# A fifth output tile beside the first four in the output projections behind the mixers, and wider spacing of the last heads of the differential attention

## The chip, the cores and the metric

The kernel runs on one core of one Trainium2 chip. The metric is the device time of one execution in microseconds (us). Each time below is the median of several executions; the time before is the median of 3, 1430.43 us (1430.12 to 1432.36).

## The reference

A stack of two transformer layers and one hybrid layer on 256 tokens of width 1024, in float32. The first two layers put 16 meta tokens in front, so that they work on 272 rows. Cut to what matters here:

```python
for i in range(2):                                    # 272 rows
    h = h + 0.5 * rmsnorm(swiglu(rmsnorm(h, g[0]), ...), g[1])
    m = neighborhood_attention(...) if i == 0 else diff_attention(...)
    h = h + rmsnorm(m, g[3])                          # m = concat(heads) @ w_o
    h = h + 0.5 * rmsnorm(swiglu(rmsnorm(h, g[4]), ...), g[5])
x = h[:, 16:]
x = x + rms_norm(concat(attention, mlstm) @ w_out, g_mix_post)
x = x + rms_norm(square(relu(rms_norm(x, g) @ w_up)) @ w_down, g_mlp_post)
```

Each of the three mixers (neighbourhood attention, differential attention, and attention beside an mLSTM) ends in a 1024 x 1024 output projection, followed by an RMS norm over the row and by the next layer's up projection. These three projections are what the change touches.

## The kernel before, in words

Activations lie transposed, as eight blocks of 128 features by 272 (or 256) token columns. A weight matrix comes from HBM in pieces of 1 MB (256 output columns), three of which fit in the ring of raw pieces `wr`. Each piece makes two parts of 128 columns. A part is split into two float32r halves: ScalarE copies it (`wh`, L156), VectorE subtracts the copy from the raw piece (`wl`, L168). Seven parts can be held. `mm3` (L390 to L395) multiplies one 128-row block of one part with one block of the activations in three matmuls (high with high, high with low, low with high), a triple below; an output tile of the projection is eight triples in one PSUM accumulator `pm`.

The order in every queue is the order in which the code is written (`tc.manual_schedule()`); `Weights.pump` (L180) puts the splits between the other work, and `low` (L162) issues the next 1 MB transfer on SyncE's queue as soon as both parts of a raw piece are split. `high` (L137) refuses a part that is more than seven beyond the last part given back by `W.done`.

While a mixer's projections run, the attention is a generator in `bg_list`; each `bg()` runs it up to its next `yield`. `proj_out` (L688) starts before the attention has ended: it takes four output tiles at once and goes over the eight blocks of the attention's output (`Oh`, `Ol`) as these become ready, two `bg()` per block. Then it evacuates the four tiles (two ScalarE instructions each, the square for the norm, L379 or L387, and the scaled copy, L603 or L606; VectorE adds up the squares, L388) and does tiles 4 to 7 one after the other with `gemm`, each evacuated behind its matmuls. `pump` calls stand between the evacuations. At the end `post.finish` (L609) makes the row's 1/rms: sums over partitions on TensorE (L344), two small VectorE steps, a power on GpSimd (L349), transposes on TensorE; `start_phase` (L465) fills TensorE meanwhile with matmuls whose result is not used (L476, twice nine).

In the differential attention `da_attention` (L1204) unit u is one of 16 pairs of head and query tile; behind unit 15 the loop has four more turns for the work that is left: `values(u-3)` (L1240), `scale(u-3)` (L1253, VectorE), and `emit` (L1259 to L1261), which transposes a head's two scaled tiles and writes `Oh` and `Ol`. In these four turns each step has one `yield`.

Of the kernel before, what the change touches and what calls it, by code (L numbers as in the profile page):

```python
# [79 lines left out]
class Weights:  # L80
# [111 lines left out]
    def next(self):  # L192
        p = self.n_next
        while self.n_split <= p:
            if self.n_high <= p:
                before = self.n_high
                self.high()
                assert self.n_high > before
            self.low()
        self.n_next += 1  # L200
        return self.parts[p]
# [8 lines left out]
def block_kernel(ctx: ExitStack, tc: tile.TileContext, a, out):  # L210
# [13 lines left out]
    def nm(s):  # L224
        uid[0] += 1
        return f"{s}_{uid[0]}"
# [13 lines left out]
    def keep():  # L240
        ring_next[0] = (ring_next[0] + 1) % len(ring_blocks)
        return ring_blocks[ring_next[0]]

    def small(shape, s="s"):
        n = int(np.prod(shape[1:]))
        return tp.tile(shape, F32, name=nm(s), tag="s4" if n <= 4 else "s64", bufs=40 if n <= 4 else 6)

    def ps_mm():
        return pp.tile([128, T], F32, name=nm("pm"), tag="mm", bufs=6)

    def ps_s(shape=(128, T)):
        return pp.tile(list(shape), F32, name=nm("ps"), tag="mm", bufs=6)

    def ps_t(shape=(128, T)):
        return pp.tile(list(shape), F32, name=nm("pt"), tag="t", bufs=2)


    W = Weights(nc, wp)
# [53 lines left out]
    x = a["x"][0].rearrange("(t p) f -> p t f", p=128)  # L312
# [77 lines left out]
    def mm3(ps, w, k, x, j, cols, start, stop):  # L390
        wh, wl = w
        xh, xl = x
        pe.matmul(ps, wh[:, k, :], xh[:, j, cols], start=start, stop=False)  # L393
        pe.matmul(ps, wh[:, k, :], xl[:, j, cols], start=False, stop=False)  # L394
        pe.matmul(ps, wl[:, k, :], xh[:, j, cols], start=False, stop=stop)  # L395
# [4 lines left out]
    def bg(n=1):  # L400
        for _ in range(n):
            while bg_list:
                try:
                    next(bg_list[0])
                    break
                except StopIteration:
                    bg_list.pop(0)

    def gemm(ps, x, cols, kb=8, start=True, stop=True, inside={}):
        w = W.next()  # L410
        for k in range(kb):
            mm3(ps[:, cols], w, k, x, k, cols, start and k == 0, stop and k == kb - 1)
            if k in inside:
                inside[k]()
            if k in bg_at[0]:
                bg()
        W.done()
# [269 lines left out]

    def proj_out(post, x, order=range(8)):  # L688

        c = post.cols  # L690
        w = [W.next() for _ in range(4)]
        ps = [ps_mm() for _ in range(4)]
        for n, k in enumerate(order):
            while k not in ready:
                assert bg_list
                bg()
            W.flush()
            for q in range(4):
                mm3(ps[q][:, c], w[q], k, x, k, c, n == 0, n == 7)
                if q % 2:  # L700
                    bg()
        while bg_list:
            bg()
        bg_at[0] = (3,)
        ready.clear()
        W.done(4)
        for q in range(4):
            post.evac(ps[q], q)
            if q % 2:
                W.pump(1 if q == 1 else 2)  # L710
        for j in range(4, 8):
            p = ps_mm()
            gemm(p, x, c)
            post.evac(p, j)
            if j < 6:
                W.pump()
# [200 lines left out]
    def softmax(ps, parts, n, sm):  # L917


        lg, mn = tmp("lg"), 3.0e38  # L920
        for cols, bias in parts:
            hi, mn = mn, small([128, 1])
            dve.tensor_tensor_reduce(out=lg[:, cols], in0=ps[:, cols], in1=bias, scale=-1.0, scalar=hi,
                                     op0=OP.add, op1=OP.min, accum_out=mn)
        e = keep()
        act.activation(e[:, 0:n], lg[:, 0:n], AF.Exp, bias=mn, scale=-1.0, accum_out=sm)
        return e
# [40 lines left out]
    def available(n):  # L968

        while progress["units"] <= n:  # L970
            yield
# [226 lines left out]
    def token_rms(o):  # L1198

        q, ss = tmp("osq"), small([128, 1])  # L1200
        act.activation(q[:, 0:128], o, AF.Square, accum_out=ss)
        return ss

    def da_attention():  # L1204

        vp, A, AT, OS, normed, sums, first = {}, {}, {}, {}, {}, {}, {}

        def scores(u):
            hd, qt = divmod(u, 2)
            A[u] = []  # L1210
            sums[u] = small([128, 2])
            for s in range(2):
                ps = ps_s()
                pe.matmul(ps, kq[64 * s:64 * s + 64, hd % 4, QT[qt]], kq[64 * s:64 * s + 64, 4 + hd % 4, :],
                          start=True, stop=True)
                u0 = 128 * (1 - qt)
                A[u].append(softmax(ps, [(ALL, t5b[hd // 4][:, hd % 4, u0:u0 + T])], T, sums[u][:, s:s + 1]))

        def weights(u):
            e0, e1 = A[u]  # L1220
            sm, r, x = sums.pop(u), small([128, 2]), small([128, 1])
            dve.reciprocal(r, sm)
            dve.scalar_tensor_tensor(x, r[:, 1:2], sm[:, 0:1], nlam, op0=OP.mult, op1=OP.mult)
            dve.scalar_tensor_tensor(e0, e1, x, e0, op0=OP.mult, op1=OP.add)
            A[u], first[u] = e0, r[:, 0:1]

        def turn(u):
            if u % 2 == 0:
                AT[u // 2] = ring[0].tile().rearrange("p (t k q) -> p t k q", t=2, k=3)
            q = A.pop(u)  # L1230
            p = ps_t((128, 3, 128))
            for i, x in enumerate((0, 128, 144)):
                pe.transpose(p[:, i, :], q[:, x:x + 128], ident)
            act.activation(AT[u // 2][:, u % 2], p, AF.Copy)

        def values(u):
            hd, qt = divmod(u, 2)
            o = ps_s((128, 128))
            for k in range(3):
                pe.matmul(o, AT[hd][:, qt, k, :], vp[hd][:, k, :], start=k == 0, stop=k == 2)  # L1240
            ss = token_rms(o)
            m, r, r0 = small([128, 1]), small([128, 1]), first.pop(u)
            dve.scalar_tensor_tensor(m, ss, r0, r0, op0=OP.mult, op1=OP.mult)
            dve.tensor_scalar(m, m, 1.0 / 128, EPS, op0=OP.mult, op1=OP.add)
            pool.tensor_tensor(r, m, mhalf[:, 0:1], op=OP.pow)
            normed[u] = o, r0, r

        def scale(u):
            hd, qt = divmod(u, 2)
            o, r0, r = normed.pop(u)  # L1250
            if qt == 0:
                OS[hd] = keep()
            dve.tensor_scalar(OS[hd][:, qt * 128:qt * 128 + 128], o, r0, r, op0=OP.mult, op1=OP.mult)  # L1253

        def emit(hd):
            p = ps_t((128, 256))
            t = OS.pop(hd)
            for qt in range(2):
                pe.transpose(p[:, qt * 128:qt * 128 + 128], t[:, qt * 128:qt * 128 + 128], ident)  # L1259
            act.activation(Oh[:, hd, GRID], p, AF.Copy, scale=gsub)  # L1260
            dve.scalar_tensor_tensor(Ol[:, hd, GRID], p, gsub, Oh[:, hd, GRID].bitcast(F32),  # L1261
                                     op0=OP.mult, op1=OP.subtract)
            ready.add(hd)

        def turn_v(hd):
            vp[hd] = vp_ring[hd % len(vp_ring)]
            transpose_pair(vp[hd], vT.pop(hd))

        def v_step(u):
            if u % 2 == 0 and 2 <= u < 18:  # L1270
                while u // 2 - 1 not in vT:
                    yield
                turn_v(u // 2 - 1)

        for u in range(16 + 4):
            if u % 2 and u >= 5:
                emit((u - 5) // 2)
            if 3 <= u < 19:
                values(u - 3)
            if 2 <= u < 18:  # L1280
                turn(u - 2)
            yield
            if u < 16:
                yield from available(u)
                scores(u)
                yield
            yield from v_step(u)
            if 3 <= u < 19:
                scale(u - 3)
            if u < 16:  # L1290
                weights(u)
                yield

    mixer(norm, post, da_evac, da_attention, GRID, lambda n: None)
    post = Post(gains(1, 3), GRID)
# [22 lines left out]
    c = GRID  # L1318
# [355 lines left out]
    for n in range(2):  # L1674
        ps = [ps_s((128, 512)) for _ in range(2)]
        for i in range(12 if n else 16):
            w = W.next()
# [9 lines left out]
    w = [W.next() for _ in range(4)]  # L1687
# [34 lines left out]
```

## Time and profile before

| | |
|---|---|
| median of 3 executions | 1430.43 us |
| the profiled execution | 1431.22 us, of which its span 1429.4 us |
| TensorE matmul busy | 1408.2 us (99%) |
| VectorE, ScalarE, GpSimd busy | 893.7, 750.2, 168.1 us |
| mean granted TensorE clock | 0.998 of full speed |
| moved by DMA | 234.41 MB, mean 164 GB/s |

TensorE has matmuls in nearly every stretch, but its busy time contains the matmuls that only fill it (L476). An engine's row in the timeline shows start, length, line, operation, out<-in, and in brackets the idle time before it and what released it. The three projections run from 328 to 358 us (272 columns, neighbourhood attention), 877 to 907 us (256 columns, differential attention) and, in the hybrid layer, up to 1236 us (256 columns).

### The profile page before, as it was taken

How to read it: one execution, taken by the hardware profiler on the slowest of the kernel's cores; microseconds unless marked ns; L12 is line 12 of the kernel's file. 1: busy time of each engine (PE TensorE's matmuls, PEld its weight loads, DVE VectorE, ACT ScalarE, POOL GpSimd, SP SyncE). 2: the span in 40 equal slices, each digit the busy share in tenths (PEclk: the TensorE clock that was granted, in tenths of full speed). 3: DMA queues.
4: the chain of work that ended last, by engine and by line, in shares of the span. 5: the costliest groups of instructions: out<-in, count | busy, mean ns of one | idle time of the engine just before them, and what ended most of it. 6: DMA issues, size and time to landing. Idle time of an engine off the chain costs nothing.

```text
span 1429.4 us, 26895 instructions
## 1 busy us (share of the span) xinstructions
PE 1408.2 (99%) x11068; PEld 1357.6 (95%) x11068; DVE 893.7 (63%) x1668; ACT 750.2 (52%) x1333; POOL 168.1 (12%) x185
## 2 busy tenths in 40 slices
PE   9999999999999999999999999999999999999997
PEld 9999999899999999999999888999999888899886
DVE  6776447664865544955546785776555877686542
ACT  5554346666554444644445564664444565676441
POOL 1325001010221200212100001031100000000000
PEclk9999999999999999999999999999999999999999
DMA  7875552352575554555553352375554543275650
GB/s 250 271 251 172 179 185 66 124 167 90 167 229 172 168 180 148 175 180 177 163 182 99 119 177 89 112 244 184 188 178 131 177 129 108 89 234 179 221 177 30
DMA packets 219528, 234.41 MB, mean 164 GB/s; under 512 B 5313, under 2 KB 209894, under 8 KB 219214
## 3 DMA queue, kind: packets, MB, share of 16 engines
q1 hardware_dynamic: 218206, 227.38, 49.2%
q0 software_dynamic: 656, 4.94, 1.1%
q8 instruction: 87, 1.43, 0.4%
q10 hardware_dynamic: 544, 0.38, 0.1%
q14 instruction: 35, 0.29, 0.1%
HBM read 231.62 MB, written 5.13 MB: 166 GB/s over the span
## 4 chain that ended last, share of the span: by engine, by line
PE 91%; DVE 6%; ACT 2%; DMA 1%; issue 1%; POOL 0%; DVEq 0%; POOLq 0%; ACTq 0%; SPq 0%
PE pm L393 24%; PE pm L395 24%; PE pm L394 23%; PE ps L1645 2%; PE ps L1644 2%; PE ps L1646 2%; PE pm L506 2%; DVE wl L168 2%; PE pm L502 2%; PE pm L503 1%; DMA wr<-in_da_w_qkv_dram 1%; PE pt L344 1%; PE pt L1013 1%; PE pm L540 1%; PE ps L1022 1%
## 5 line engine op out<-in xcount | busy, mean ns | idle before, releaser
L168 DVE TENSOR_TENSOR wl<-wr,wh 128x1024 fp32r<-128x1024 f32 (+1 forms) x430 | 514.3, 1204 | 122.9 <-ACT wh L156 122.2
L393 PE MATMUL pm<-xh,wh 128*128 128x272 f32 (+1 forms) x1992 | 581.4, 292 | 2.2 <-DVE Ol L421 2.2
L395 PE MATMUL pm<-xh,wl 128*128 128x272 f32 (+1 forms) x1992 | 570.4, 286 | 0.0
L394 PE MATMUL pm<-xl,wh 128*128 128x272 f32 (+1 forms) x1992 | 568.5, 285 | 0.0
L156 ACT ACTIVATE wh<-wr 128x1024 fp32r<-128x1024 f32 (+1 forms) x430 | 440.7, 1033 | 194.0 <-PE pm L394 112.9
L393 PEld LDWEIGHTS pm<-xh,wh 128*128 128x128 f32 x1992 | 376.0, 189 | 11.2 <-issue 9.4
L395 PEld LDWEIGHTS pm<-xh,wl 128*128 128x128 f32 x1992 | 375.9, 189 | 0.1
L394 PEld LDWEIGHTS pm<-xl,wh 128*128 128x128 f32 x1992 | 375.6, 189 | 0.1
L395 PE MATMUL pm<-mh,wl 128*128 128x272 f32 (+1 forms) x704 | 202.2, 287 | 0.0
L393 PE MATMUL pm<-mh,wh 128*128 128x272 f32 (+1 forms) x704 | 202.1, 287 | 0.0
L394 PE MATMUL pm<-ml,wh 128*128 128x272 f32 (+1 forms) x704 | 201.5, 286 | 0.0
L650 POOL TENSOR_TENSOR sr<-sl,rb 128x272 f32<-128x272 f32 (+1 forms) x88 | 104.5, 1192 | 320.1 <-ACT sl L648 320.1
L395 PEld LDWEIGHTS pm<-mh,wl 128*128 128x128 f32 x704 | 132.7, 188 | 0.0
L394 PEld LDWEIGHTS pm<-ml,wh 128*128 128x128 f32 x704 | 132.6, 188 | 0.0
L393 PEld LDWEIGHTS pm<-mh,wh 128*128 128x128 f32 x704 | 132.6, 188 | 0.0
L420 ACT ACTIVATE mh<-m 128x272 fp32r<-128x272 f32 (+1 forms) x88 | 37.7, 428 | 117.8 <-DVE m L655 117.6
L655 DVE TENSOR_TENSOR m<-pm,sr 128x272 f32<-128x272 f32 (+1 forms) x88 | 38.3, 435 | 80.5 <-PE pm L395 74.8
L648 ACT ACTIVATE sl<-gq 128x272 f32<-128x272 f32 (+1 forms) x88 | 36.9, 427 | 95.8 <-DVE gq L646 95.6
L349 POOL TENSOR_TENSOR s<-s,mhalf 128x3 f32<-128x3 f32 (+1 forms) x15 | 19.1, 1274 | 558.4 <-DVE s L362 336.1
L646 DVE TENSOR_TENSOR gq<-pm,rb 128x272 f32<-128x272 f32 (+1 forms) x88 | 37.6, 435 | 71.6 <-PE pm L395 69.0
L388 DVE TENSOR_TENSOR accf<-accf,sq 128x272 f32<-128x272 f32 (+1 forms) x42 | 18.3, 436 | 81.9 <-ACT sq L387 81.8
L502 PE MATMUL pm<-xh,wh 128*128 128x272 f32 (+1 forms) x224 | 56.7, 291 | 0.6
(337 smaller groups left out, 1728.6 us busy)
## 6 DMA issues: line engine op xcount, KB each, us to landing
wr<-in_ffn_w_gate_dram SPq DMA_DIRECT2D x43, 1024.0 KB
wr<-in_ffn_w_up_dram SPq DMA_DIRECT2D x43, 1024.0 KB
wr<-in_ffn_w_down_dram SPq DMA_DIRECT2D x32, 1024.0 KB
wr<-in_w_up_dram SPq DMA_DIRECT2D x16, 1024.0 KB
wr<-in_w_down_dram SPq DMA_DIRECT2D x16, 1024.0 KB
wr<-in_ffn_w_down_dram SPq DMA_DIRECT2D x16, 768.0 KB
wr<-in_na_w_qkv_dram SPq DMA_DIRECT2D x12, 1024.0 KB
wr<-in_da_w_qkv_dram SPq DMA_DIRECT2D x12, 1024.0 KB
```

The source lines that it names most:

```text
L156: self.nc.scalar.activation(hi, w, AF.Copy)
L168: engine.tensor_tensor(lo, w, hi.bitcast(F32), op=OP.subtract)
L393: pe.matmul(ps, wh[:, k, :], xh[:, j, cols], start=start, stop=False)
L394: pe.matmul(ps, wh[:, k, :], xl[:, j, cols], start=False, stop=False)
L395: pe.matmul(ps, wl[:, k, :], xh[:, j, cols], start=False, stop=stop)
L420: act.activation(hi, src, AF.Copy)
L502: pe.matmul(ps[q][:, c], w[q][0][:, k, :], norm.xh[:, k, c], start=k == 0, stop=False)
L506: pe.matmul(ps[q][:, c], w[q][0][:, k, :], norm.xl[:, k, c], start=False, stop=k == 7)
L646: dve.tensor_tensor(t[:, c], ps[:, c], norm.rb[:, c], op=OP.mult)
L648: act.activation(s[:, c], t[:, c], AF.Silu)
L650: pool.tensor_tensor(s2[:, c], s[:, c], norm.rb[:, c], op=OP.mult)
L655: dve.tensor_tensor(t[:, c], ps[:, c], gated.pop(f)[:, c], op=OP.mult)
```

## The change

Two edits. In `proj_out`, before the last of the eight blocks is waited for, a fifth tile is opened and takes its first seven blocks in a row; the last block then goes through five tiles. Five tiles are evacuated together, three follow alone. The `pump` behind the second evacuation splits two parts where it split one, and one `pump` more stands behind the fifth. In `da_attention` the turns u = 16 and u = 18 give 1 and 3 more `yield`s.

```diff
@@ proj_out
         for n, k in enumerate(order):
+            if n == 7:
+                w.append(W.next())
+                ps.append(ps_mm())
+                for i, j in enumerate(order[0:7]):
+                    mm3(ps[4][:, c], w[4], j, x, j, c, i == 0, False)
+                    bg()
             while k not in ready:
                 assert bg_list
                 bg()
             W.flush()
-            for q in range(4):
+            for q in range(len(ps)):
                 mm3(ps[q][:, c], w[q], k, x, k, c, n == 0, n == 7)
...
-        W.done(4)
-        for q in range(4):
+        W.done(5)
+        for q in range(5):
             post.evac(ps[q], q)
             if q % 2:
-                W.pump(1 if q == 1 else 2)
-        for j in range(4, 8):
+                W.pump(2)
+            elif q == 4:
+                W.pump()
+        for j in range(5, 8):
             p = ps_mm()
             gemm(p, x, c)
             post.evac(p, j)
@@ da_attention
             if u < 16:
                 weights(u)
                 yield
+            else:
+                for _ in range({16: 1, 18: 3}.get(u, 0)):
+                    yield
```

No instruction is added or taken away on any engine; GpSimd and SyncE keep their order as well. ScalarE, at the end of the first projection, before: `accf` and `sq` are squares of tiles, `f` their scaled copies, `wh` splits; wr_3854 is the last piece of the projection's own weight, wr_3953 and wr_4110 the first two pieces of the next layer.

```order
L387 ACTIVATE sq_4304<-pm_4125,V 128x272
L606 ACTIVATE f_4122<-pm_4125,gbo,G 128x272
L156 ACTIVATE wh_4309<-wr_3854 128x1024
L387 ACTIVATE sq_4312<-pm_4126,V 128x272
L606 ACTIVATE f_4122<-pm_4126,gbo,G 128x272
L387 ACTIVATE sq_4316<-pm_4127,V 128x272
L606 ACTIVATE f_4122<-pm_4127,gbo,G 128x272
L156 ACTIVATE wh_4323<-wr_3953 128x1024
L156 ACTIVATE wh_4326<-wr_3953 128x1024
```

The same stretch now:

```order
L387 ACTIVATE sq_4329<-pm_4125,V 128x272
L606 ACTIVATE f_4122<-pm_4125,gbo,G 128x272
L156 ACTIVATE wh_4334<-wr_3854 128x1024
L156 ACTIVATE wh_4337<-wr_3953 128x1024
L387 ACTIVATE sq_4340<-pm_4126,V 128x272
L606 ACTIVATE f_4122<-pm_4126,gbo,G 128x272
L387 ACTIVATE sq_4344<-pm_4127,V 128x272
L606 ACTIVATE f_4122<-pm_4127,gbo,G 128x272
```

One more split stands ahead of the third and the fourth evacuation. Behind the evacuation of the sixth tile there stands, before and now, one split of the next layer's third piece (wr_4321, now wr_4349) and then the last two evacuations; ScalarE now:

```order
L387 ACTIVATE sq_4394<-pm_4369,V 128x272
L606 ACTIVATE f_4122<-pm_4369,gbo,G 128x272
L156 ACTIVATE wh_4401<-wr_4349 128x1024
L387 ACTIVATE sq_4429<-pm_4404,V 128x272
L606 ACTIVATE f_4122<-pm_4404,gbo,G 128x272
L385 ACTIVATE sq_4464<-pm_4433,V 128x128
```

On TensorE, behind the last piece of attention work in the differential projection, the last head's transposes stood ahead of the fourth block's triples, before:

```order
L1240 MATMUL ps_10687<-vs_9154,ring_9343 128x128 x3
L393 MATMUL pm_10589<-Oh_9150,wh_10328 128x256
L394 MATMUL pm_10589<-Ol_9151,wh_10328 128x256
L395 MATMUL pm_10589<-Oh_9150,wl_10329 128x256
L393 MATMUL pm_10590<-Oh_9150,wh_10358 128x256
L394 MATMUL pm_10590<-Ol_9151,wh_10358 128x256
L395 MATMUL pm_10590<-Oh_9150,wl_10359 128x256
L1259 MATMUL pt_10706<-ident,keep_9153 128x128 x2
L393 MATMUL pm_10587<-Oh_9150,wh_10205 128x256
```

Now eight triples (the fourth and fifth block through four tiles) lie between those values (L1240, now L1249) and the transposes (L1259, now L1268), of which the last triple stands here:

```order
L393 MATMUL pm_10590<-Oh_9150,wh_10358 128x256
L394 MATMUL pm_10590<-Ol_9151,wh_10358 128x256
L395 MATMUL pm_10590<-Oh_9150,wl_10359 128x256
L1268 MATMUL pt_10730<-ident,keep_9153 128x128 x2
L393 MATMUL pm_10587<-Oh_9150,wh_10205 128x256
```

The transposes of the head before it moved in the same way behind two triples.

## Rows read from the trace of the kernel before

**Rows 1.** The page, part 1: busy time, share of span, instructions.

```profile
PE 1408.2 (99%) x11068; PEld 1357.6 (95%) x11068; DVE 893.7 (63%) x1668; ACT 750.2 (52%) x1333; POOL 168.1 (12%) x185
```

**Rows 2.** Waits of PE: total us, times, longest.

```profile
PE pt L1259 <- DVE keep L1253: 1.9, 2, 1.3
PE pm L393 <- ACT Oh L420: 0.5, 1, 0.5
```

**Rows 3.** Timeline, PE, differential projection: two waits, then two triples eight apart.

```profile
883.08 0.33 PE L1259 MATMUL pt<-ident,keep 128*128 128x128 f32 x1 [0.61 <-DVE keep L1253]
...
888.04 0.33 PE L1259 MATMUL pt<-ident,keep 128*128 128x128 f32 x1 [1.30 <-DVE keep L1253]
...
898.13 0.28 PE L393 MATMUL pm<-Oh,wh 128*128 128x256 f32 x1
...
900.97 0.28 PE L393 MATMUL pm<-Oh,wh 128*128 128x256 f32 x1
```

**Rows 4.** Timeline, PE, hybrid projection, start of its last block.

```profile
1222.49 0.39 PE L393 MATMUL pm<-Oh,wh 128*128 128x256 f32 x1 [0.48 <-ACT Oh L420]
1222.95 0.39 PE L394 MATMUL pm<-Ol,wh 128*128 128x256 f32 x1
```

**Rows 5.** Timeline, PE, first projection: two triples eight apart, sums behind it.

```profile
340.04 0.28 PE L393 MATMUL pm<-Oh,wh 128*128 128x272 f32 x1
...
343.07 0.28 PE L393 MATMUL pm<-Oh,wh 128*128 128x272 f32 x1
...
357.79 0.72 PE L344 MATMUL pt<-ones,accf 128*128 128x1 f32 x6
```

**Rows 6.** Timeline, ACT, end of the first projection.

```profile
344.77 0.49 ACT L379 ACTIVATE accf<-pm,V 128x272 f32<-128x272 f32 x1 [6.96 <-PE pm L395]
...
346.45 1.07 ACT L156 ACTIVATE wh<-wr 128x1024 fp32r<-128x1024 f32 x1
347.40 0.50 ACT L387 ACTIVATE sq<-pm,V 128x272 f32<-128x272 f32 x1
...
348.24 0.52 ACT L387 ACTIVATE sq<-pm,V 128x272 f32<-128x272 f32 x1
...
355.56 1.06 ACT L156 ACTIVATE wh<-wr 128x1024 fp32r<-128x1024 f32 x1 [0.86 <-DMA wr<-in_ffn_w_gate_dram]
356.53 0.47 ACT L387 ACTIVATE sq<-pm,V 128x272 f32<-128x272 f32 x1
...
357.99 0.64 ACT L385 ACTIVATE sq<-pm,V 128x128 f32<-128x128 f32 x2 [0.52 <-PE pm L395]
```

**Rows 7.** Timeline, DVE and SP, the same stretch.

```profile
349.14 1.22 DVE L168 TENSOR_TENSOR wl<-wr,wh 128x1024 fp32r<-128x1024 f32 x1
...
350.43 0.37 SPq L105 DMA_DIRECT2D wr<-in_ffn_w_gate_dram  x1
```

**Rows 8.** Timeline, ACT, end of the differential projection.

```profile
904.44 1.06 ACT L156 ACTIVATE wh<-wr 128x1024 fp32r<-128x1024 f32 x1 [1.35 <-DMA wr<-in_ffn_w_gate_dram]
...
906.85 0.45 ACT L385 ACTIVATE sq<-pm 128x128 f32<-128x128 f32 x2 [0.71 <-PE pm L395]
```

**Rows 9.** Timeline, ACT, end of the hybrid projection.

```profile
1233.82 1.06 ACT L156 ACTIVATE wh<-wr 128x1024 fp32r<-128x1024 f32 x1 [1.65 <-DMA wr<-in_w_up_dram]
...
1235.92 0.45 ACT L385 ACTIVATE sq<-pm 128x128 f32<-128x128 f32 x2 [0.41 <-PE pm L395]
```

**Rows 10.** Timeline, PE, inside the neighbourhood attention, behind its longest wait.

```profile
270.64 0.36 PE L393 MATMUL pm<-xh,wh 128*128 128x272 f32 x1 [2.19 <-DVE Ol L421]
270.84 0.28 PE L394 MATMUL pm<-xl,wh 128*128 128x272 f32 x1
```

**Rows 11.** Windows: stretch, busy us (count) per engine; last granted clock, DMA share, GB/s.

```profile
272.00:274.00 2.00, 2.00 (x12) 1.97 (x10) 0.72 (x4) 0.90 (x3) 0.00 (x0) 0.50 1.01 346
274.00:276.00 2.00, 2.00 (x13) 1.93 (x13) 0.00 (x0) 0.30 (x1) 0.00 (x0) 0.65 0.02 4
888.00:890.00 2.00, 1.96 (x17) 1.96 (x18) 0.48 (x1) 0.47 (x1) 0.00 (x0) 1.00 0.00 0
```

## Prediction

> **What bounds the kernel now.** I read the page's busy times first, then the waits of TensorE, then the three projections in the timeline, engine by engine. TensorE is busy 1408.2 of 1429.4 us [rows 1], so all that better filling could give is some 21 us, and each place has to be priced by itself. Two of its waits lie in the changed code: 1.91 us in the last transposes of the differential attention, as 0.61 and 1.30 us, and 0.48 us ahead of the hybrid projection's last block [rows 2 to 4]. The first projection, behind the neighbourhood attention, has no wait at its last block.
>
> The second thing to see is ScalarE at the ends of the three projections. It stands still from the attention's last work until the first four tiles are complete (6.96 us in the first projection), and from there to the end it hardly rests [rows 6]. Near the end it waits for a transfer, with a split of the next layer's third weight piece: 0.86, 1.35 and 1.65 us in the three projections [rows 6, 8, 9]. The last evacuation is behind that split in its queue. It comes just in time: ScalarE has been idle for 0.52, 0.71 and 0.41 us when the last tile is complete [rows 6, 8, 9]. What follows (square, sums, power, transposes, the next layer) is a chain in which TensorE only has filling to do. So the last evacuation is on the path that sets the end, and its reserve is about half a microsecond.
>
> **What the change gives.** No instruction is added or removed, so no work is priced, only order. (a) The differential attention's yields put two triples ahead of the first waiting transposes and eight ahead of the second. A triple of 256 columns is (900.97 - 898.13) / 8 = 0.355 us [rows 3], so the covers are 0.7 and 2.8 us against waits of 0.61 and 1.30. Both waits go: -1.91 us. The scaling that was waited for hangs on values that TensorE computes no later than now. What is next late would be `Oh` and `Ol` of the last head; behind its transposes there still lie two blocks through four tiles and the fifth tile's seven triples, 15 x 0.355 = 5.3 us, enough for two operations of half a microsecond. (b) In the hybrid projection the fifth tile stands in the wait for the last head: seven triples, 2.49 us, against 0.48 us, and against the second matmul's lag, which starts 0.46 us behind the first where 0.20 us is the distance after another wait [rows 4, 10]. I take -0.48 - 0.26 = -0.74 us; the ends are 0.48 and 0.74. (c) The first projection has nothing to cover there: 0. Together -2.65 us.
>
> **What the change costs.** The fifth tile's seven triples stand in front of the last block, so the first four tiles are complete seven triples later, while the last tile is not: the sum of the triples is the same. ScalarE's whole queue starts that much later. At 272 columns a triple is (343.07 - 340.04) / 8 = 0.379 us, so it is 2.65 us in the first projection and 2.49 us in the two others [rows 3, 5].
>
> What then follows is rigid, and I go through it in the first projection. The fourth tile's square (348.24) lets VectorE add it up and then do the low half of the projection's last part (349.14); with that done, SyncE can issue the next piece into the freed buffer (350.43); ScalarE has it at 355.56, 5.13 us later [rows 6, 7]. So the split that waits is 7.32 us behind the fourth square. The change puts one more split ahead of the third tile's evacuation: 347.40 - 346.45 = 0.95 us [rows 6]. Waiting split and last two evacuations are therefore late by 2.65 + 0.95 us, less the 0.52 us reserve: 3.08 us behind the last tile's completion. Queued behind that split are the last two evacuations on ScalarE, behind these the last addition of squares on VectorE, the sums on TensorE and the whole norm; nothing of the next layer can start without it. The same in the differential projection: 2.49 + 0.95 - 0.71 = 2.73 us, and in the hybrid one 2.49 + 0.95 - 0.41 = 3.03 us [rows 8, 9]. Lower bound of each is 0 (the transfer is no longer what ends last), upper bound with reserve spent is 3.60, 3.44 and 3.44 us; I take the middle values, since each step has its row.
>
> Net per projection: +3.08; 2.73 - 1.91 = +0.82; 3.03 - 0.74 = +2.29. Sum +6.2 us. The extra `pump` behind the fifth tile splits one part and changes no count. Of PSUM's six accumulators five are then open; the sixth is free for tile 5, and tile 6 needs the first one's evacuation, done long before: nothing. SyncE's queue holds only the weight pieces here, in the same order; the next two are issued later by less than the layer itself, so I add nothing.
>
> The Trainium skill, Perfetto Trace Analysis, section Matmuls, says that independent groups of matmuls should rotate through banks so that one group's evacuation overlaps the next group's matmuls. The change goes against it: five tiles end together and three tiles' matmuls are left to cover their evacuation, where four were. By that rule alone the price is ScalarE's queue without the transfer, which is the third case below.
>
> **The clock.** TensorE then stands still for about 3 us at each of the three ends, from the last tile to the sums, which stood directly behind it before (357.79) [rows 5]. Its longest wait now is 2.19 us, and behind that one the granted clock fell to half: 0.50 and 0.65 in two windows of 2 us, which is 1.0 + 0.7 = 1.7 us of full-speed work lost; behind the 1.30 us wait it stayed at 1.00 [rows 10, 11]. Half here is 1.2 of 2.4 GHz. Three us is nearer to the wait that cost the clock. What it costs lies between 0 (the slow stretch falls on filling or waiting) and 1.7 us per end, or twice that if the thin work after the gap keeps it low; the filling between sums and transposes is on the path as soon as it takes twice its time, so I take 1.2 us for each end: +3.6 us.
>
> The Trainium skill, TensorE: Matmul & The Clock Gate, section Why this matters for your kernels, advises against idle gaps between bursts of matmuls, because the clock falls back. [...]
>
> **The rivals.** (1) Forecast: waits for the transfer at all three ends and the clock falls there. The profiled execution takes 1431.22 us with a span of 1429.4; the median of the shown runs is 0.8 us below, and I add to the median: 1430.4 + 6.2 + 3.6 = 1440.2 us. (2) The same waits, but the clock holds, as behind the wait of 1.30 us: 1436.6 us. (3) Not slower: the transfer lands earlier, as it is alone in its queue when issued. It decides from about 2 us less than the 5.13 us measured; then only ScalarE's own queue is late. In the first projection seven evacuations of 0.84 us (347.40 to 348.24) and six splits of 0.95 us are 11.6 us, and TensorE has 357.99 - 344.77 - 2.65 = 10.6 us left: +1.0 us; in the narrower two I take 0. That gives 1430.4 - 2.65 + 1.0 = 1428.8 us. Against it speaks that the transfer was alone in its stretch before as well. (4) The yields do not do what they say: the scaling moves along with the transposes and the 1.9 us stay; with the rest of (1) 1442.1 us. The order speaks against it. (5) The clock stays low for two stretches at each end, 3 x 3.4 instead of 3.6: 1446.8 us.
>
> **How the numbers follow.** Chances: (1) 0.50, (2) 0.26, (3) 0.10, (4) 0.06, (5) 0.08. The time is that of (1). The range 1435.0 to 1442.5 holds (1), (2) and most of (4), with the two unknown sizes in it (clock 0 to 1.4 per end, the waits by half a us each); (3) and (5) are left out. A measurement of this kernel can tell about 0.2%, 2.9 us, from no change. Faster than 1427.6 needs (3) without its backlog: 0.02. Within is (3) and a little of (2): 0.10. The rest, 0.88, is slower.
>
> **What will show it.** In the profile after, ScalarE should wait some 2.5 to 3.5 us for the weight transfer ahead of the sixth split at each end, where it waited 0.86 to 1.65, and TensorE should stand idle about 3 us ahead of the L344 sums there; these would be new rows among TensorE's waits. The waits on the transposes should be gone. The granted clock should show a window near 0.5 behind each of the three gaps. The prediction is wrong if ScalarE's last evacuation starts with the last tile as it does now, if the transfer of the third piece is issued no later than before against the end of TensorE's work, or if the time is below 1433 us.

## The result and the profile after

The changed kernel takes 1444.02 us (median of 4 executions, 1440.49 to 1444.35) against 1430.28 us before: a ratio of 1.0088 with a 95% interval of 1.0076 to 1.0100, some 13.7 us slower. The sign and the mechanism were predicted; the size was not, and the time lies above the upper end of the range, 1442.5 us. The profiled execution took 1444.19 us with a span of 1442.4 us, 13.0 us more than the span before.

One word on the change itself. The `pump` behind the fifth tile is not one more: before, the loop over tiles 4 to 7 had it there, behind tile 4. It split two parts then and splits one now, so one split has moved from behind the fifth tile to behind the second, and ScalarE splits as much as before. (The prediction, too, speaks of an extra `pump`; its count of the splits stands.)

The page of the changed kernel, part 1: the busy times answer to [rows 1]. The work is the same; TensorE is "busy" 6 us longer although no matmul was added, which is a first hint that some of them run slowly.

```profile
PE 1414.2 (98%) x11068; PEld 1365.7 (95%) x11068; DVE 893.0 (62%) x1668; ACT 749.7 (52%) x1333; POOL 168.9 (12%) x185
```

TensorE's waits in the changed kernel (total us, times, longest) answer to [rows 2]. The waits on L1259 (now L1268) and on `Oh` are gone; a new one stands three times ahead of the sums of squares. The second line, a wait of 2.19 us inside the neighbourhood attention, was there before ([rows 10]).

```profile
PE pt L344 <- DVE accf L388: 10.3, 3, 3.5
PE pm L393 <- DVE Ol L421: 2.2, 1, 2.2
```

The end of the first projection, TensorE (start, length, instruction, idle time before it and its releaser). The last tile's last matmul starts at 356.34, the sums follow at 360.00; before, they followed at once [rows 5]. The next layer's first matmul (L502) is the third row.

```profile
356.34 0.29 PE L395 MATMUL pm<-Oh,wl 128*128 128x272 f32 x1
360.00 1.44 PE L344 MATMUL pt<-ones,accf 128*128 128x1 f32 x6 [3.38 <-DVE accf L388]
367.43 0.43 PE L502 MATMUL pm<-xh,wh 128*128 128x272 f32 x1
```

The same stretch on ScalarE and SyncE, as [rows 6] and [rows 7]. The evacuations begin at 346.10, the transfer is issued at 352.71, the split that needs it stands still for 2.01 us (0.86 before) and starts 5.33 us after the issue. The last evacuation, which had waited for TensorE before, starts 3.2 us behind the last tile. What TensorE waits for is the addition of the squares of the tile before (VectorE, L388), whose evacuation stands directly behind that split.

```profile
346.10 0.49 ACT L379 ACTIVATE accf<-pm,V 128x272 f32<-128x272 f32 x1 [9.61 <-PE pm L395]
...
358.04 1.06 ACT L156 ACTIVATE wh<-wr 128x1024 fp32r<-128x1024 f32 x1 [2.01 <-DMA wr<-in_ffn_w_gate_dram]
359.00 0.47 ACT L387 ACTIVATE sq<-pm,V 128x272 f32<-128x272 f32 x1
...
359.84 0.63 ACT L385 ACTIVATE sq<-pm,V 128x128 f32<-128x128 f32 x2
```

```profile
352.71 0.37 SPq L105 DMA_DIRECT2D wr<-in_ffn_w_gate_dram  x1
```

The two other ends look the same. ScalarE in the differential and in the hybrid projection, as [rows 8] and [rows 9]:

```profile
911.19 1.06 ACT L156 ACTIVATE wh<-wr 128x1024 fp32r<-128x1024 f32 x1 [2.77 <-DMA wr<-in_ffn_w_gate_dram]
...
912.77 0.44 ACT L385 ACTIVATE sq<-pm 128x128 f32<-128x128 f32 x2
...
1244.85 1.06 ACT L156 ACTIVATE wh<-wr 128x1024 fp32r<-128x1024 f32 x1 [2.86 <-DMA wr<-in_w_up_dram]
```

TensorE there: idle time, sums, and the first matmul of the next layer.

```profile
913.12 0.98 PE L344 MATMUL pt<-ones,accf 128*128 128x1 f32 x4 [3.45 <-DVE accf L388]
...
918.91 0.28 PE L502 MATMUL pm<-xh,wh 128*128 128x256 f32 x1
...
1246.69 1.01 PE L344 MATMUL pt<-ones,accf 128*128 128x1 f32 x4 [3.45 <-DVE accf L388]
...
1252.82 0.36 PE L502 MATMUL pm<-xh,wh 128*128 128x256 f32 x1
```

The same instructions in the kernel before, for the distance from the sums to the next layer:

```profile
362.24 0.39 PE L502 MATMUL pm<-xh,wh 128*128 128x272 f32 x1
...
906.65 0.50 PE L344 MATMUL pt<-ones,accf 128*128 128x1 f32 x4
...
910.41 0.38 PE L502 MATMUL pm<-xh,wh 128*128 128x256 f32 x1
...
1235.73 0.54 PE L344 MATMUL pt<-ones,accf 128*128 128x1 f32 x4
...
1239.44 0.39 PE L502 MATMUL pm<-xh,wh 128*128 128x256 f32 x1
```

From the first sum (357.79 in [rows 5]) to the next layer it took 4.45, 3.76 and 3.71 us; now it takes 7.43, 5.79 and 6.13 us, so 2.98, 2.03 and 2.42 us more for the same instructions, together 7.4 us. The windows of the changed kernel show why (stretch, busy us and count of each engine; last the granted clock, DMA share, GB/s). At the first end the clock falls in the idle time and is at half, 1.2 of 2.4 GHz, until the next layer has begun.

```profile
358.00:360.00 2.00, 0.00 (x0) 0.00 (x0) 0.44 (x1) 1.96 (x4) 0.00 (x0) 0.68 1.10 360
360.00:362.00 2.00, 2.00 (x10) 2.00 (x10) 0.16 (x1) 1.75 (x5) 0.00 (x0) 0.50 1.10 348
...
366.00:368.00 2.00, 2.00 (x11) 2.00 (x11) 1.76 (x5) 0.00 (x0) 0.00 (x0) 0.50 0.00 0
368.00:370.00 2.00, 2.00 (x15) 2.00 (x13) 1.93 (x6) 1.05 (x2) 0.00 (x0) 0.76 0.00 0
```

The difference of the spans, put together from the two traces: +10.3 us of idle time at the three ends, and +0.5 us because the sums used to start 0.16 us before the last matmul's end; +7.4 us of half clock in the chains behind; -3.1 us of gains (2.2 in the differential projection, 0.9 in the hybrid one); -1.3 us ahead of the first end; -0.8 us in small shifts between the layers. That is 13.0. The -1.3 us are 1.6 us from the wait of 2.19 us behind which the clock had fallen before [rows 10, 11], less 0.3 us lost elsewhere. The changed kernel has the same wait, and the clock holds behind it:

```profile
272.00:274.00 2.00, 2.00 (x19) 2.00 (x18) 0.96 (x5) 1.18 (x4) 0.00 (x0) 1.00 1.08 375
```

So the dip from which the prediction took the price of the clock comes and goes with the same wait. All thirteen profiled executions (both kernels and the runs below) have this wait, of 2.18 to 2.19 us; the clock fell behind it in six of them and held in seven, and with the yields alone it stayed low about twice as long as in [rows 11]:

```profile
272.00:274.00 2.00, 2.00 (x11) 1.92 (x11) 1.00 (x5) 0.63 (x3) 0.00 (x0) 0.50 1.08 375
274.00:276.00 2.00, 2.00 (x10) 2.00 (x10) 0.00 (x0) 0.59 (x1) 0.00 (x0) 0.50 0.12 31
276.00:278.00 2.00, 2.00 (x14) 1.78 (x13) 0.04 (x1) 0.59 (x1) 0.00 (x0) 0.72 0.00 0
```

### The profile page after: what moved, and what is told of

It reads as the page before. It is cut to its first block, busy times and chain, and to the rows that moved or that the text cites. A ratio compares the mean times of both kernels' runs of the same rounds, so it can differ in the third digit from the quotient of the medians.

```text
span 1442.4 us, 26895 instructions
## 1 busy us (share of the span) xinstructions
PE 1414.2 (98%) x11068; PEld 1365.7 (95%) x11068; DVE 893.0 (62%) x1668; ACT 749.7 (52%) x1333; POOL 168.9 (12%) x185
## 3 DMA queue, kind: packets, MB, share of 16 engines
HBM read 231.62 MB, written 5.13 MB: 164 GB/s over the span
## 4 chain that ended last, share of the span: by engine, by line
PE 90%; DVE 5%; ACT 2%; DMA 1%; issue 1%; POOL 0%; POOLq 0%; DVEq 0%; SPq 0%; ACTq 0%
PE pm L393 24%; PE pm L395 23%; PE pm L394 23%; PE ps L1657 2%; PE ps L1656 2%; PE ps L1658 2%; DVE wl L168 2%; PE pm L506 2%; PE pm L502 2%; PE pm L503 2%; PE pm L476 1%; PE pt L344 1%; DMA wr<-in_ffn_w_gate_dram 1%; PE ps L1249 1%; ACT wh L156 1%; PE pm L540 1%
## 5 line engine op out<-in xcount | busy, mean ns | idle before, releaser
L388 DVE TENSOR_TENSOR accf<-accf,sq 128x272 f32<-128x272 f32 (+1 forms) x42 | 18.2, 434 | 89.8 <-ACT sq L387 89.8
L502 PE MATMUL pm<-xh,wh 128*128 128x272 f32 (+1 forms) x224 | 56.8, 292 | 0.3
```

Of the source, the lines that this page charges most:

```text
L502: pe.matmul(ps[q][:, c], w[q][0][:, k, :], norm.xh[:, k, c], start=k == 0, stop=False)
```

## Experiments

Theory: an end costs twice. TensorE waits there for the last evacuations, which stand behind a split that waits for its transfer; and the idle time brings the clock down for the chain that follows. Rivals: the yields or the fifth tile cost something elsewhere; the clock only falls where it costs nothing; ScalarE's queue is too long without any transfer.

**The yields alone.** The kernel before, with

```diff
             if u < 16:
                 weights(u)
                 yield
+            else:
+                for _ in range({16: 1, 18: 3}.get(u, 0)):
+                    yield
```

> The kernel before with the new yields of the differential attention alone; no fifth tile anywhere. Theory (the change's loss lies at the ends of the three projections, its gain in the yields): the two waits of TensorE for the scaled heads, 0.61 and 1.30 us in the trace of before, go and nothing takes their place: 1430.3 - 1.9 = 1428.4 us, a ratio of about 0.9987. Rival (the yields only work together with the fifth tile's background steps, or the spread pushes other steps late): 1430.3 us or above. If the whole loss of the change came from the yields, 1444.

Measured: 1428.57 us, ratio 0.9984 (0.9974 to 0.9994). The yields gain about 2 us, as expected; the loss is not theirs.

**The same wait with TensorE kept at work.** The changed kernel, with

```diff
             gemm(p, x, c)
+            if j == 7:
+                d, y = ps_mm(), flat(W.parts[W.n_next][0])[:, 0:256]
+                for _ in range(24):
+                    pe.matmul(d[:, 0:256], y[:, 0:128], y, start=True, stop=True)
             post.evac(p, j)
```

> The changed kernel with 24 matmuls of 256 columns, whose result nobody reads, behind the last block's matmuls of each of the three projections and ahead of the row sums: about 24 x 0.13 = 3.1 us of work where TensorE stands idle for 3.38, 3.45 and 3.45 us. They take no work away and shorten no wait. Theory (about half of the loss is the clock, which falls to half after the idle time and stays there through the row sums and the chain to the first matmul of the next part; by the offsets of the two traces 3.28, 1.77 and 2.10 us at the three ends): the granted clock stays at 1.00 and 7.15 us come back: 1444.0 - 7.2 = 1436.8 us. Rival (the half clock lies beside waits of the chain that take as long at full clock, so the idle time alone is the loss): no change, 1444, or a little above for matmuls that end late.

Measured: 1436.28 us, ratio 1.0033 (1.0022 to 1.0045). Some 7.7 us come back although no wait was made shorter; the two intervals leave some 2.4 us of doubt on that difference. TensorE at the second end, and its windows:

```profile
908.64 3.03 PE L726 MATMUL pm<-wh 128*128 128x256 f32 x24
912.06 0.58 PE L344 MATMUL pt<-ones,accf 128*128 128x1 f32 x4 [0.39 <-DVE accf L388]
```

```profile
908.00:912.00 4.00, 3.67 (x31) 3.47 (x29) 2.30 (x4) 1.88 (x5) 0.00 (x0) 1.00 1.09 358
912.00:916.00 4.00, 3.91 (x30) 3.61 (x31) 1.55 (x5) 1.30 (x4) 0.70 (x1) 1.00 0.90 285
```

The sums still start 3.4 us behind the last tile (3.03 + 0.39), but take 0.58 us where they took 0.98, and the clock stays at 1.00. So it does at the third end. At the first end the clock fell even so, behind an idle time of 0.36 us, and the chain took 5.44 us, 1.0 more than before. What is left over the kernel before, 1436.28 - 1430.6 (its median in the same comparison) = 5.7 us, is therefore the waits less the gains, and about 1 us of half clock.

**The split behind the last evacuation.** The changed kernel, with

```diff
-            if j < 6:
-                W.pump()
+            if j == 6:
+                W.low_if()
+            elif j == 7:
+                W.high()
```

> The changed kernel with one split of each projection moved: the high half of the first part of the third 1 MB piece of the next weights, which stood on ScalarE behind the evacuation of block 5, now stands behind that of block 7, and the low half that stood behind the sum of block 5 on VectorE stands behind that of block 6. Work and transfers are the same. Theory (the evacuations of blocks 6 and 7 stand in ScalarE's queue behind a split whose transfer lands late): the three idle times of TensorE fall from 3.4 us to about 0.8 (what VectorE's queue ahead of the sum leaves), the clock holds: the yields' 1.9 and the hybrid projection's 0.7 remain as gains, 1430.3 - 2.6 + 3 x 0.8 = 1430.1 us. Rival (the transfer is needed soon anyway: the next part's first matmuls or the gain activations behind the split then wait for it): the loss moves behind the chain, 1436 to 1444.

Measured: 1429.19 us, ratio 0.9985 (0.9975 to 0.9996): the whole loss is gone. TensorE's waits, and ScalarE at the second end:

```profile
PE pt L344 <- DVE accf L388: 2.0, 3, 0.8
```

```profile
906.37 0.45 ACT L385 ACTIVATE sq<-pm 128x128 f32<-128x128 f32 x2 [0.64 <-PE pm L395]
906.70 0.48 ACT L603 ACTIVATE f<-pm,G 128x256 f32<-128x256 f32 x1
907.60 1.06 ACT L156 ACTIVATE wh<-wr 128x1024 fp32r<-128x1024 f32 x1 [0.42 <-DMA wr<-in_ffn_w_gate_dram]
```

The last evacuation waits for TensorE again, as in [rows 8], and the split waits for its transfer behind it, where nobody is held up. So neither the fifth tile nor the length of ScalarE's queue costs the time; the place of one 1 us instruction in that queue does. (The edit also moves one low half on VectorE behind the next sum of squares; that is nearer to the end, not further from it.) The clock still fell at the first end, behind 0.84 us.

**The transfer earlier, the queue unchanged.** The changed kernel, with

```diff
             if q % 2:
                 W.pump(2)
+                if q == 1:
+                    W.low()
             elif q == 4:
```

> The changed kernel with the low half of the last part of the output weights taken at once behind the second block's evacuation instead of behind the fourth's; this frees the 1 MB piece some 2.0 to 2.4 us earlier and so sends the transfer earlier. ScalarE's order is the changed kernel's. Theory: the split behind block 5 waits 0, 0.8 and 0.9 us in place of 2.01, 2.77 and 2.86; TensorE's three idle times fall from 3.4 us to about 1.5, since the split itself still stands ahead of the last two evacuations. With the clock holding through 1.5 us, 1430.3 - 2.6 + 3 x 1.5 = 1432.2 us; with the clock falling as before it, 1439. Rival (the transfer is not what decides, but ScalarE's longer queue of splits): no change, 1444.

Measured: 1434.47 us, ratio 1.0026 (1.0015 to 1.0038), between the two values. The idle times fell about as far as expected (to 1.78, 1.63 and 1.39 us), but the clock fell behind all three. TensorE's waits, and the split at the second end:

```profile
PE pt L344 <- DVE accf L388: 4.8, 3, 1.8
```

```profile
908.25 1.06 ACT L156 ACTIVATE wh<-wr 128x1024 fp32r<-128x1024 f32 x1 [0.95 <-DMA wr<-in_ffn_w_gate_dram]
```

**One split ahead of the fourth evacuation instead of two.** The changed kernel, with

```diff
             if q % 2:
-                W.pump(2)
+                W.pump(1 if q == 1 else 2)
```

> The changed kernel with one split of the next weights in place of two behind the second block's evacuation of each projection, as the kernel before has it; the second comes behind the fourth, so ScalarE does the same work in all. Theory (a split of 0.95 us ahead of the fourth evacuation puts off the low half that frees the 1 MB piece, and with it the transfer that ends the wait): the transfer leaves 0.95 to 1.05 us earlier at each end, TensorE's three idle times fall from 3.4 to about 2.4 us, the clock falls as in the changed kernel: 1444.0 - 3.0 = 1441.0 us. Rival (the extra split only fills time in which ScalarE waits anyway): no change, 1444.

Measured: 1439.36 us, ratio 1.0060 (1.0041 to 1.0079). The gain is larger than expected, and the time alone does not show that the extra split is on the path, because the clock's part was smaller too: in the profiled execution the chains are 1.1, 1.1 and 1.2 us longer than before, where the changed kernel's were 2.98, 2.03 and 2.42. The idle times show it at two ends, 2.28 and 2.14 us in place of 3.45. At the first end the transfer left 0.9 us earlier (351.80) but the split started 6.6 us behind it instead of 5.3, so that end gained nothing (3.71 us). ScalarE there:

```profile
358.42 1.06 ACT L156 ACTIVATE wh<-wr 128x1024 fp32r<-128x1024 f32 x1 [2.35 <-DMA wr<-in_ffn_w_gate_dram]
```

**The fifth tile in the first projection alone.** The kernel before, with `proj_out5` (the changed `proj_out`) beside the old one:

```diff
@@ first projection
-    proj_out(post, (Oh, Ol))
+    proj_out5(post, (Oh, Ol))
```

> The kernel before with the fifth tile in the first projection alone (272 columns), without the new yields; the two others as in the kernel before. Theory (each projection's end costs for itself: 3.4 us of idle time and, by the offsets of the traces, 3.3 us of half clock at this end): 1430.3 + 6.7 = 1437.0 us. Were the clock's part 1.2 us, as the prediction had it: 1434.9. Rival (the loss comes about only where ends follow each other, or at the differential one, whose order the yields change): 1430.3 to 1432.

Measured: 1436.19 us, ratio 1.0041 (1.0028 to 1.0055), from 1432.59 to 1438.30. One end costs 4.9 us over the 1431.31 us of before in this comparison: on its own, without the others, and more than the 3.51 us of its idle time. It fits 1.2 us of clock (+4.6 by the expectation) better than 3.3 (+6.7); the spread holds both. The profiled execution is the shortest of the six, with a chain 1.1 us longer than before and a mean granted clock of 0.998; in the four longest the clock was 0.994 to 0.996.

**The change without its yields.** The changed kernel, with

```diff
-            else:
-                for _ in range({16: 1, 18: 3}.get(u, 0)):
-                    yield
```

> The changed kernel without the new yields: the fifth tile in all three projections. Theory (yields and fifth tile add up: the two waits of 0.61 and 1.30 us for the scaled heads come back): 1444.0 + 1.9 = 1445.9 us. Rival (the seven triples of the fifth tile, which stand ahead of the last block, cover the second of these waits on their own, so the yields bring 0.6 at most): 1444.0 to 1444.6.

Measured: 1441.87 us, ratio 1.0083 (1.0064 to 1.0103): 2.2 us below the changed kernel, where 1.9 above was expected. Its trace has the waits on the transposes back (1.9 us) but less half clock at the ends: from the sums to the next layer 1.1, 1.1 and 2.4 us over before. So I ran both again, and this kernel with the filler too.

**Changed kernel, and change without yields, once more** (no further edit; the second is the kernel above).

> The changed kernel once more, beside its version without the yields on the same chip. Two theories on the clock's part at the three ends, which the traces so far show as 1.1 us (one stretch at half clock) or 2 to 3.3 us (two and more) behind idle times of the same length. If two stretches belong to this kernel's ends, the median is 1444.0 us again and the executions lie close together. If it is drawn anew in each execution, the executions spread over 1438 to 1445 us and the median falls to about 1442.

> The changed kernel without the new yields, in more executions: it came out at 1441.87 us where 1445.9 was expected, 2.2 us below the changed kernel, though its trace has the two waits of 0.6 and 1.3 us back. If the yields still bring 1.9 us and only the clock's part was drawn differently, the median lies 1 to 2.5 us above that of the changed kernel in this comparison. If the yields cost something where the fifth tile is, it lies below again.

Measured: 1443.91 us (1441.77 to 1444.01), ratio 1.0084 (1.0070 to 1.0097), and 1445.09 us (1441.48 to 1447.87), ratio 1.0094 (1.0080 to 1.0109). The order is the expected one now, with overlapping intervals. Of the two theories on the clock neither holds alone: the changed kernel's median is the same again, but its new profile has 2.97, 1.09 and 2.16 us of longer chains where the first had 2.98, 2.03 and 2.42, and the second kernel's executions lie 6 us apart. The differential end of the changed kernel in its new profile, to be held against 913.12 and 918.91 above:

```profile
914.07 0.58 PE L344 MATMUL pt<-ones,accf 128*128 128x1 f32 x4 [3.31 <-DVE accf L388]
...
918.92 0.28 PE L502 MATMUL pm<-xh,wh 128*128 128x256 f32 x1
```

The shortest of the second kernel's executions is the profiled one, and its windows at the first end, to be held against those of the changed kernel above, show the clock below full in three rows of 2 us instead of six, behind an idle time of 3.2 us:

```profile
360.00:362.00 2.00, 1.86 (x16) 1.86 (x17) 0.41 (x3) 1.90 (x6) 0.01 (x1) 0.97 1.10 348
362.00:364.00 2.00, 2.00 (x12) 2.00 (x11) 0.00 (x0) 0.00 (x0) 0.85 (x1) 0.50 0.80 251
364.00:366.00 2.00, 2.00 (x13) 2.00 (x14) 1.60 (x4) 0.00 (x0) 0.00 (x0) 0.68 0.00 0
366.00:368.00 2.00, 2.00 (x19) 2.00 (x18) 1.93 (x6) 0.66 (x2) 0.00 (x0) 1.00 0.00 0
```

**The change without yields, with the filler.** The two diffs above together.

> The changed kernel without the new yields and with the 24 matmuls in the idle time of each of the three ends, so that the clock's part is left out of the comparison. If the yields bring 1.9 us beside the fifth tile too: 1436.3 + 1.9 = 1438.2 us. If the fifth tile's triples cover these waits: 1436.3 to 1436.9.

Measured: 1440.33 us, ratio 1.0063 (1.0049 to 1.0077). By the ratios it lies 0.30% = 4.3 us above the filler kernel with yields, more than 1.9; that is a comparison across chips with intervals of 2 us each. In the traces the two lie 2.7 us apart at the end, 2.3 of it in the differential projection. The time is above both expected values; in the traces the yields bring a little more than the 1.9 us that were predicted, beside the fifth tile too. Against the same kernel without filler the difference is 1445.09 - 1440.33 = 4.8 us: the clock's part again, smaller than the 7.7 us above, with up to 3 us of doubt.

**What may gain, put together.** The kernel before with the yields, and in the hybrid projection alone the fifth tile with the late split:

```diff
+            else:
+                for _ in range({16: 1, 18: 3}.get(u, 0)):
+                    yield
...
-    proj_out(post, (Oh, Ol), [4, 5, 6, 7, 0, 1, 2, 3])
+    proj_out5(post, (Oh, Ol), [4, 5, 6, 7, 0, 1, 2, 3])
@@ proj_out5, from the changed proj_out
-            if j < 6:
-                W.pump()
+            if j == 6:
+                W.low_if()
+            elif j == 7:
+                W.high()
```

> The parts that may bring a gain put together: the kernel before with the new yields, and the fifth tile in the hybrid projection alone, there with the late split behind the last evacuation and its low half behind the seventh sum. Theory: 1.9 us of the yields and 0.74 us of the wait for the last head go, against 0.5 us that the sum of the seventh block is late at the hybrid end: 1430.3 - 2.1 = 1428.2 us. Rival (the fifth tile brings nothing even where its wait is taken away): 1428.6 or above, as with the yields alone.

Measured: 1427.82 us, ratio 0.9982 (0.9971 to 0.9993). It beats both kernels; from the yields alone (0.9984) it cannot be told apart, so no run shows in its time that the fifth tile brings anything.

## Why the prediction was wrong in size

- **The yields (-1.91 us): right.** The waits are gone, nothing took their place, and alone they bring about 2 us. In the changed kernel's trace the differential projection gains 2.2 us.
- **The fifth tile in the hybrid projection (-0.74 us): right as far as the trace goes.** Just ahead of the last block TensorE runs 8.2 us later than before, at the end of the last tile 7.3 us later: 0.9 us were gained.
- **The waits at the ends (3.08, 2.73, 3.03 us): right in their cause, somewhat small in size.** The last evacuation starts 3.2, 3.1 and 3.2 us after TensorE's idle time begins; before, it started 0.2 us after the first sum (357.79 and 357.99 in [rows 5, 6]), so it is 3.0, 2.9 and 3.0 us late, as the sum had it. But TensorE waits for the squares of the tile before, which had some 0.3 us of reserve and not the 0.41 to 0.71 of the sum: the sums start 3.5, 3.6 and 3.6 us later against the last tile, 10.8 in all where 8.8 were predicted, near the upper bounds that the prediction gave. The cause is the one named: the late start, the extra split, the transfer, with 5.3 to 5.7 us from its issue to the split. The late split shows that ScalarE's order is what turns it into a loss. Waits less gains were predicted as 6.2 us; the filler kernel leaves 5.7 (with 1 us of clock in it), the trace of the changed kernel has 7.7 (10.8 - 3.1). The Trainium skill, Perfetto Trace Analysis, section Tensor Engine Instruction, calls ScalarE's and VectorE's execution strictly first in, first out; the trace agrees: the last two evacuations stood behind a split that waited 2.0 to 2.9 us for its data, the last of them with its tile complete for over 3 us.
- **The clock (3 x 1.2 = 3.6 us): the step that failed.** That the clock falls was right; the price was too low. It was taken from one place, the dip behind the 2.19 us wait [rows 10, 11], put at 1.7 us there and lowered to 1.2. That row was one outcome of several: in other executions the same wait cost nothing, or about twice as much. And at the ends there follow single-column sums, filling and transposes, all of it on the path; at the first end six rows of 2 us lie below full clock. The filler kernel measured the term as 7.7 us (4.8 us in the second pair), and the trace of the changed kernel has 7.4 us of longer chains (6.2 in its second profile), not 3.6. That 1430.4 + 6.2 + 7.7 comes to 1444.3 is no proof of its own, since 7.7 is itself a difference from the measured 1444.0. The prediction had this as its rival of two slow stretches, 1446.8 us with a chance of 0.08, and left it out of the range. Its own rows did not decide between one stretch and two, and such a term belongs in the range with both ends. In a single execution 3.6 us can come out nearly: the shortest one without the yields has 3.1 us of longer chains.
- **That the clock holds behind a short wait was read too widely,** from one wait of 1.30 us [rows 11]. In the kernel with the early low half it fell behind 1.78, 1.63 and 1.39 us, and with the late split behind 0.84 us at the first end, while it held behind 0.62 and 0.52 us at the two others.
- The rival by which the transfer lands earlier is refuted for these runs (the split starts 5.1 to 6.6 us behind the issue, 5.13 to 5.42 before), and so is that of yields that move nothing.

## What to carry to other kernels

When work is put ahead of a shared step, follow what each engine's queue holds behind that step: an instruction that waits for a transfer delays all that stands behind it, and moving that one instruction behind the urgent ones can be worth more than the change itself. If a change opens an idle gap on TensorE ahead of a thin chain, price the gap twice, as waiting and as half clock through the chain, and let the range hold one slow stretch and several. Do not take the price from one dip in one trace: see whether the clock falls at that place in other executions too. Filling matmuls that cover such a gap separate the two parts in one run.

## What the runs showed of the hardware

The same idle time costs differently from execution to execution. In all 19 places in these traces where TensorE stood idle for 1.4 to 3.7 us ahead of the sums, the clock fell to half. The chain from the sums to the next layer then took between 0.8 and 3.0 us longer than before, at the same place in the same kernel too: at the differential end of the changed kernel 2.03 us in one profiled execution and 1.09 in the other. The length of the idle time does not decide it: at the first end 1.78 us cost 2.7 us of chain (early low half) and 3.71 us cost 1.1 (one split). TensorE there, in these two runs:

```profile
358.40 1.36 PE L344 MATMUL pt<-ones,accf 128*128 128x1 f32 x6 [1.78 <-DVE accf L388]
...
365.58 0.29 PE L502 MATMUL pm<-xh,wh 128*128 128x272 f32 x1
```

```profile
360.38 0.83 PE L344 MATMUL pt<-ones,accf 128*128 128x1 f32 x6 [3.71 <-DVE accf L388]
...
365.97 0.29 PE L502 MATMUL pm<-xh,wh 128*128 128x272 f32 x1
```

This is part of why one kernel's times spread. The kernel with the late split shows it best: its four longest executions, 1430.0 to 1431.3 us, have a mean granted clock of 0.996, the six others, 1427.3 to 1429.3 us, one of 0.998 or 0.999. For the kernel before (1427.7 to 1433.9 us in 27 executions) the two go together only loosely. The Trainium skill, TensorE: Matmul & The Clock Gate, Part 1 (The HAM clock gate), says of the start of a kernel that the number of matmuls at the low clock is "run-variable" for one and the same kernel; these traces show the like in the middle of one. What decides between a short and a long slow stretch here stays open; no run varied that alone. The first projection's end was the most sensitive one: in the three kernels that had less than 1 us of idle time at all three ends (late split and both with the filler) the clock fell there, behind 0.84, 0.36 and 0.65 us, and held at the two others, behind 0.33 to 0.62 us. It costs each about 1 us.
